# Hybrid SSD and differential-attention layer on one core: two short pauses written into TensorE's planned order

## The chip, the cores and the metric

The kernel runs on one core of a Trainium2 chip: TensorE (matmuls, its weight loads listed apart), VectorE, ScalarE, GpSimd (POOL) and the DMA queues, of which SyncE issues nearly all. The metric is the device time of one execution in microseconds; the time of a kernel is the median of its runs.

## The reference

One encoder layer over x (1024 tokens x 1024 features, float32). After a layer norm h, one projection gives z, x/B/C, step sizes, q, k, v and a gate g (6688 columns). One branch is a bidirectional Mamba-2 scan with a gated RMS norm. The other is differential attention, 8 heads, two softmax maps per head, value width 128:

```
scores = einsum(q, k) * 64**-0.5 - slope[h] * |t - s|
w      = softmax(map 0) - lam * softmax(map 1)
o      = einsum(w, v)                                   # (tokens, 8, 128)
o      = rms_norm(o, subln_g) * (1 - lam_init) * silu(g)
```

Both branches are joined, projected by w_out (2048 x 1024), added to 2**0.25 * h and layer-normed.

## The kernel before

Products of float32 accuracy are made of three float32r products, of high and low parts: hi*hi, hi*lo, lo*hi. All of TensorE's instructions are issued in one order that a small planner, the class `Loom`, works out while the program is built. Each piece of work is a generator, a lane; `LANES` (line 29) gives it a rank and a margin. What a lane yields says when it wants to go on:

- tiles: when the planner's model has them ready, plus the lane's margin;
- a function: when it is true;
- a float: that long after TensorE's planned free time.

`run` (line 103) takes the lane that is due first; of those due by TensorE's planned time, the one with the lowest rank. The model counts 512 x 0.000417 + 0.003 us for a 512-column float32r product and 0.107 for a transpose. Only TensorE's order is pinned by it in this stage: the order of VectorE, ScalarE and GpSimd, and the place of each tile in its pool, are made by the framework's own scheduler from the program.

The attention stage runs from about 420 to 1110 us. Its lanes:

- `fill` (rank 9): the input projection. A block is 128 output columns; for each half of the tokens (512) it accumulates 8 triples of products in one PSUM bank, yielding between triples. The head's blocks come as q, k, v, gate, head after head, so that the projections of later heads fill TensorE between the pieces of the attention of earlier ones.
- `scores` (rank 4): for a block of 128 queries, four products of 512 columns for the two maps and four with the low part of k, to two PSUM tiles of their own pool (`a_s`); VectorE then adds the distance term and finds the minimum, ScalarE takes the exponential.
- `combine` (4.125): the two maps are scaled and subtracted, on POOL and VectorE.
- `values` (4.25): the map (tile `p`) is transposed in two groups of four, each into a bank, copied as high part `wh` (ScalarE) and low part `wl` (VectorE); after every second block of queries 24 products with the values follow. Only when a block's second group has been split does the lane let `scores` go on.
- `v_tail` (rank 3, margin 0.4; lines 935 to 943): a half of a v block is copied from its bank to `vc` by ScalarE; this lane transposes it in four pieces into a bank, from which ScalarE makes `vh` and VectorE `vl`.
- `finish` (4.2, margin 2; lines 1070 to 1100): once per head and half of the tokens, the RMS norm of `o`. ScalarE squares `o`, the square is split in `osh` and `osl`, two products with ones sum it over the 128 partitions into a bank (`pms`), VectorE reads the bank into `msq`, ScalarE takes logarithm and exponential (`rt`), VectorE polishes, and `o` goes to DRAM by four DMAs. `done` counts the halves; it frees the gate buffers of the head before last, and for head 6 it opens the pool of the output projection.

The banks: `bank` (line 247) takes one of four PSUM banks (tag `bk`). `fill`, `values`, `v_tail` and `finish` all use it; the lanes ask for their bank before they yield for it. The last stage, `project_out`, begins in the last head's attention, when the input projection has no blocks left.

Of the kernel before, what the change touches and what calls it, by code (L numbers as in the profile page):

```python
# [216 lines left out]
def hybrid_layer_kernel(  # L217
# [29 lines left out]
    def bank(shape=(128, 512)):  # L247
        return pm.tile(shape, F32, name="bk", bufs=4)

    def dma(dst, src):  # L250
        SP.dma_start(dst, src)

    def transpose(dst, src, n=128):
        T.transpose(dst, src, ident[:n, :n])
# [630 lines left out]
    heads_ = [Head(h) for h in range(8)]  # L885

    def free_since(h, what, n):

        if h == 0 and what != "done":
            return None  # L890
        if h < 2:
            return lambda: state["open"]
        return lambda: getattr(heads_[h - 2], what) == n
# [31 lines left out]
    def proj_v(h):  # L925
        H = heads_[h]

        def evac(half, ps):
            if half == 0:
                H.vh = H.pool().tile([128, NCH, 128], F32R, name="vh")  # L930
                H.vl = H.pool().tile([128, NCH, 128], F32R, name="vl")
            vc = (att["ap"] if h else late["sq"]).tile([128, 512], F32, name="vc", tag="zr", bufs=2)
            A.copy(vc, ps)

            def tail():
                pt = bank((128, 4, 128))
                yield (vc, pt)
                for j in range(4):
                    transpose(pt[:, j, :], vc[:, 128 * j:128 * j + 128])
                t = slice(4 * half, 4 * half + 4)  # L940
                A.copy(H.vh[:, t, :], pt)
                V.tensor_sub(H.vl[:, t, :], pt, H.vh[:, t, :].bitcast(F32))
                H.v += 1
            loom.add(tail(), "v_tail")
        queue.append(Block(V0 + 128 * h, evac, free_since(h, "summed", 4)))
# [87 lines left out]
    def values():  # L1033

        for _ in range(64):
# [31 lines left out]
            if n:  # L1067
                loom.add(finish(H, H.o, tb // 4))

    def finish(H, o, half):  # L1070

        h = heads_.index(H)
        osq = ap.tile([128, 512], F32, name="osq")
        A.activation(osq, o, AF.Square)
        hi = ap.tile([128, 512], F32R, name="osh", tag="rt")
        lo = ap.tile([128, 512], F32R, name="osl", tag="msq")
        A.copy(hi, osq)
        V.tensor_sub(lo, osq, hi.bitcast(F32))
        pms = bank()
        yield (lo, pms)  # L1080
        T.matmul(pms, ones_r, hi, start=True, stop=False)
        T.matmul(pms, ones_r, lo, start=False, stop=True)
        rt = ap.tile([128, 512], F32, name="rt")
        ms = ap.tile([128, 512], F32, name="msq")
        V.tensor_scalar(ms, pms, 1.0 / 128, EPS, op0=ALU.mult, op1=ALU.add)
        A.activation(rt, ms, AF.Ln)
        A.activation(rt, rt, AF.Exp, scale=-0.5)
        yield rt
        V.tensor_mul(ms, ms, rt)
        V.tensor_mul(ms, ms, rt)  # L1090
        V.tensor_scalar(ms, ms, -0.5, 1.5, op0=ALU.mult, op1=ALU.add)
        yield lambda: H.g == 1
        P.tensor_mul(o, o, H.gate[:, 512 * half:512 * half + 512])
        V.tensor_mul(rt, rt, ms)
        yield o
        V.scalar_tensor_tensor(o, o, sub8, rt, op0=ALU.mult, op1=ALU.mult)
        for j in range(4):
            dma(y_dram[4 * half + j][:, 8 + h, :], o[:, 128 * j:128 * j + 128])
        H.done += 1
# [219 lines left out]
```

## Time and profile before

| | |
|---|---|
| median of 3 runs | 1236.25 us (1234.08 to 1236.62) |
| profiled execution | 1231.77 us, its span 1230.1 us |
| mean granted TensorE clock | 0.992 |
| VectorE, ScalarE, POOL busy, share of the span | 73%, 57%, 38% |
| DMA | 98.02 MB, mean 80 GB/s |

Times are in microseconds. PE is TensorE's matmuls and PEld its weight loads, DVE VectorE, ACT ScalarE. A row of the timeline has the start, the duration, the engine, a helper's line (140 for all), the operation, `out<-in` by tile names, the shapes and the count of merged instructions; in brackets the idle time of that engine before it and what ended it. All tiles of `bank` are called `bk`, so their readers and writers tell them apart: `bk<-hh,whi`, `bk<-hl,whi` and `bk<-hh,wlo` are one triple of `fill`, `bk<-ident,vc` the transposes of v, `bk<-ident,p` those of the maps, `bk<-osh,ones_r` and `bk<-osl,ones_r` the products of the norm, `sc<-kk,q` and `sc<-kl,q` the scores. Matmuls are pipelined, so what one costs is read from one start to the next.

### The profile page before, as it was taken

Reading aid. Unit: us, or ns where it says so; the run is one execution under the profiler, and the core shown is the slowest. Engines: PE = TensorE matmul, PEld = TensorE weight load, DVE = VectorE, ACT = ScalarE, POOL = GpSimd, SP = SyncE. Lnnn points to the kernel's source line nnn. Section 1 sums busy time; section 2 is a strip of 40 time slices with the busy share of each in tenths; the row PEclk is TensorE's granted clock in tenths of the full one; section 3 lists DMA queues with packets and bytes.
Section 4 is the critical chain, followed back from the end, with each engine's and each line's share of the span. In section 5 each row is a group of like instructions: output and inputs, shape, how many; then the busy total and the mean of one; then the engine's idle time right before and its main releaser. Section 6 shows DMA issues by size and latency. Waiting matters only on the chain. (4 is left out here: it accounts for less than half of the span.)

```text
span 1230.1 us, 16472 instructions
## 1 busy us (share of the span) xinstructions
PE 1173.1 (95%) x5881; PEld 920.5 (75%) x5881; DVE 898.5 (73%) x1303; ACT 701.8 (57%) x1281; POOL 471.2 (38%) x404
## 2 busy tenths in 40 slices
PE   5999999999999999999999999999999997999997
PEld 3777667788668777778787777877777776788885
DVE  6686876767876568788788887887878888762334
ACT  4557578734577466566655657556656686552221
POOL 7412564323753223323332333233232429352354
PEclk9999999999899999999999999999999999999999
DMA  6113345622344531111111121121111263023221
GB/s 199 30 36 112 86 129 158 185 64 65 94 122 144 153 113 43 28 47 48 26 48 39 43 53 26 35 52 36 43 35 43 79 210 116 26 77 121 78 86 60
DMA packets 107590, 98.02 MB, mean 80 GB/s; under 512 B 9364, under 2 KB 79349, under 8 KB 107509
## 3 DMA queue, kind: packets, MB, share of 16 engines
q1 hardware_dynamic: 107509, 96.98, 27.4%
q8 instruction: 46, 0.75, 0.3%
q14 instruction: 35, 0.29, 0.1%
HBM read 75.85 MB, written 16.91 MB: 75 GB/s over the span
## 5 line engine op out<-in xcount | busy, mean ns | idle before, releaser
L140 PE MATMUL bk<-hh,whi 128*128 128x512 f32 x832 | 352.8, 424 | 0.9 <-DVE yt L140 0.3
L140 PE MATMUL bk<-hl,whi 128*128 128x512 f32 x832 | 327.2, 393 | 3.2 <-POOL hl L140 2.8
L140 PE MATMUL bk<-hh,wlo 128*128 128x512 f32 x832 | 328.2, 394 | 0.0
L140 ACT ACTIVATE p<-p,nm 128x1024 f32<-128x1024 f32 x128 | 146.8, 1148 | 127.7 <-DVE nm L140 126.9
L140 POOL TENSOR_TENSOR wlo<-wst,whi 128x512 fp32r<-128x512 f32 x104 | 159.0, 1534 | 144.6 <-ACT whi L140 122.2
L140 POOL TENSOR_SCALAR p<-p,rs 128x1024 f32<-128x1024 f32 x56 | 64.4, 1150 | 352.7 <-DVE rs L140 293.0
L140 PEld LDWEIGHTS bk<-hh,wlo 128*128 128x128 f32 x832 | 156.7, 188 | 35.0
L140 PEld LDWEIGHTS bk<-hh,whi 128*128 128x128 f32 x832 | 157.6, 189 | 33.1 <-issue 5.7
L140 PEld LDWEIGHTS bk<-hl,whi 128*128 128x128 f32 x832 | 157.8, 190 | 32.8 <-POOL hl L140 5.5
L140 DVE CUSTOM_DVE_ANT_0 p<-sc,dist 128x1024 f32<-128x1024 f32 x128 | 151.3, 1219 | 20.2 <-PE sc L140 19.6
L140 DVE SCALAR_TENSOR_TENSOR p<-p,rs,p 128x1024 f32<-128x1024 f32 x64 | 127.7, 1995 | 21.3 <-POOL p L140 18.0
L140 ACT CAST wh<-bk 128x512 fp32r<-128x512 f32 x128 | 74.2, 580 | 50.5 <-PE bk L140 49.9
L140 DVE TENSOR_TENSOR wl<-bk,wh 128x512 fp32r<-128x512 f32 x128 | 87.1, 684 | 15.6 <-ACT wh L140 13.6
L140 ACT CAST whi<-wst 128x512 fp32r<-128x512 f32 x104 | 64.1, 621 | 42.5 <-PE bk L140 34.3
L140 PE MATMUL bk<-ident,p 128*128 128x128 f32 x512 | 78.3, 275 | 2.6 <-ACT o L140 2.2
L140 PEld LDWEIGHTS bk<-ident,p 128*128 128x128 f32 x512 | 61.0, 140 | 26.1 <-issue 5.5
L140 ACT ACT_TABLE_LOAD x46 | 59.0, 1283 | 28.9 <-DVE t L140 17.3
L140 PE MATMUL bk<-wh,vh 128*128 128x256 f32 x256 | 74.7, 292 | 0.0
L140 PE MATMUL sc<-kk,q 128*128 128x512 f32 x256 | 72.3, 394 | 0.0
L140 PE MATMUL bk<-wl,vh 128*128 128x256 f32 x256 | 72.0, 281 | 0.0
L140 PE MATMUL bk<-wh,vl 128*128 128x256 f32 x256 | 72.0, 281 | 0.0
L140 PEld LDWEIGHTS bk<-xt,t 128*128 128x128 f32 x256 | 45.0, 190 | 24.7 <-issue 16.0
(217 smaller groups left out, 2161.3 us busy)
## 6 DMA issues: line engine op xcount, KB each, us to landing
wst<-in_w_in_dram SPq DMA_DIRECT2D x104, 256.0 KB, 3.0
t<-acs_d SPq DMA_DIRECT2D x64, 256.0 KB, 3.4
ws<-in_w_out_dram SPq DMA_DIRECT2D x32, 256.0 KB, 3.8
ys<-yd SPq DMA_DIRECT2D x32, 256.0 KB, 3.0
xb<-in_x_dram SPq DMA_DIRECT2D x8, 512.0 KB, 6.5
zd<-zs SPq DMA_DIRECT2D x16, 256.0 KB, 3.0
gz<-zd SPq DMA_DIRECT2D x16, 256.0 KB, 3.1
yd<-ys SPq DMA_DIRECT2D x16, 256.0 KB, 2.8
```

Of the source, the lines that this page charges most:

```text
L140: r = f(*args, **kw)
```

## The change

```diff
@@ -935,6 +935,7 @@
             def tail():
                 pt = bank((128, 4, 128))
                 yield (vc, pt)
+                yield 0.4
                 for j in range(4):
                     transpose(pt[:, j, :], vc[:, 128 * j:128 * j + 128])
                 t = slice(4 * half, 4 * half + 4)
@@ -1078,6 +1079,8 @@
         V.tensor_sub(lo, osq, hi.bitcast(F32))
         pms = bank()
         yield (lo, pms)
+        if H is not heads_[7]:
+            yield 0.8
         T.matmul(pms, ones_r, hi, start=True, stop=False)
         T.matmul(pms, ones_r, lo, start=False, stop=True)
         rt = ap.tile([128, 512], F32, name="rt")
```

When the lane of the transposed values has come up in the planner's order, it now steps back and is due again 0.4 us after TensorE's planned free time; so do the norm's products, with 0.8 us, in all heads but the last. Every instruction stays as it is. The program after the change holds the same instructions; TensorE's order, and with it what the scheduler makes of the other engines, can differ.

## Rows read from the trace of the kernel before

**Rows 1.** The page, part 1: busy time and share of the span.
```profile
PE 1173.1 (95%) x5881; PEld 920.5 (75%) x5881; DVE 898.5 (73%) x1303; ACT 701.8 (57%) x1281; POOL 471.2 (38%) x404
```

**Rows 2.** Sums by stretch: length, PE, PEld, DVE, ACT, POOL, granted clock, DMA.
```profile
430.00:980.00 550.00, 548.18 (x2945) 433.32 (x2944) 442.39 (x661) 334.83 (x582) 170.69 (x125) 1.00 0.18 46
...
1040.00:1046.00 6.00, 5.29 (x12) 4.02 (x13) 3.05 (x6) 0.29 (x1) 5.84 (x5) 0.50 0.16 44
```

**Rows 3.** Waits, 430 to 980: total us, times, longest.
```profile
PEld bk L140 <- ACT vc L140: 5.5, 13, 0.6
...
PEld bk L140 <- DVE osl L140: 3.7, 10, 0.5
```

**Rows 4.** Timeline, TensorE: a steady triple, transposes, and the triple behind.
```profile
476.00 0.40 PE L140 MATMUL bk<-hh,whi 128*128 128x512 f32 x1
...
476.70 0.60 PE L140 MATMUL bk<-ident,p 128*128 128x128 f32 x4
477.06 0.48 PE L140 MATMUL bk<-hh,whi 128*128 128x512 f32 x1
...
477.84 0.39 PE L140 MATMUL bk<-hh,whi 128*128 128x512 f32 x1
```

**Rows 5.** Timeline, TensorE: transposes of v, first half, head 1.
```profile
492.30 0.39 PE L140 MATMUL bk<-hh,wlo 128*128 128x512 f32 x1
...
492.82 0.42 PEld L140 LDWEIGHTS bk<-ident,vc 128*128 128x128 f32 x4 [0.56 <-ACT vc L140]
...
494.01 1.09 PE L140 MATMUL sc<-kk,q 128*128 128x512 f32 x4
```

**Rows 6.** Timeline, TensorE: around the transposes of v, second half, head 1.
```profile
502.20 0.48 PE L140 MATMUL bk<-hh,whi 128*128 128x512 f32 x1
...
504.20 1.08 PE L140 MATMUL sc<-kk,q 128*128 128x512 f32 x4
```

**Rows 7.** Timeline, TensorE: transposes of v, second half, head 7.
```profile
993.53 0.66 PE L140 MATMUL bk<-ident,vc 128*128 128x128 f32 x4 [0.57 <-ACT vc L140]
```

**Rows 8.** Timeline, TensorE: transposes of v, second half, head 0.
```profile
425.75 0.42 PEld L140 LDWEIGHTS bk<-ident,vc 128*128 128x128 f32 x4 [1.39 <-ACT vc L140]
```

**Rows 9.** Timeline, TensorE: norm products, first half, heads 0 and 1.
```profile
481.61 0.47 PE L140 MATMUL bk<-osh,ones_r 128*128 128x512 f32 x1
...
483.71 1.08 PE L140 MATMUL sc<-kk,q 128*128 128x512 f32 x4
...
561.52 0.47 PE L140 MATMUL bk<-osh,ones_r 128*128 128x512 f32 x1
...
563.50 0.86 PE L140 MATMUL sc<-kk,q 128*128 128x512 f32 x3
```

**Rows 10.** Timeline, TensorE: norm products, second half, heads 0 and 5.
```profile
521.30 0.40 PE L140 MATMUL bk<-osh,ones_r 128*128 128x512 f32 x1
...
521.77 0.19 PEld L140 LDWEIGHTS bk<-osl,ones_r 128*128 128x128 f32 x1 [0.52 <-DVE osl L140]
...
522.38 0.19 PEld L140 LDWEIGHTS bk<-hh,whi 128*128 128x128 f32 x1 [0.41 <-DVE wl L140]
...
523.18 1.09 PE L140 MATMUL sc<-kk,q 128*128 128x512 f32 x4
...
524.87 0.66 PE L140 MATMUL bk<-ident,p 128*128 128x128 f32 x4
...
920.21 0.40 PE L140 MATMUL bk<-osh,ones_r 128*128 128x512 f32 x1
...
923.71 0.55 PE L140 MATMUL bk<-ident,p 128*128 128x128 f32 x3
```

**Rows 11.** Timeline, VectorE and TensorE: a pass over the scores; the next half block.
```profile
526.12 1.22 DVE L140 CUSTOM_DVE_ANT_0 p<-sc,dist 128x1024 f32<-128x1024 f32 x1
...
530.52 0.48 PE L140 MATMUL bk<-hh,whi 128*128 128x512 f32 x1
```

**Rows 12.** Timeline, TensorE's weight loads: the longest wait for a bank.
```profile
1040.71 0.29 PEld L140 LDWEIGHTS bk<-oh,oyh 128*128 128x128 f32 x1 [4.15 <-DVE wl L140]
```

## The prediction, made before the change was run

> **What bounds the kernel now.** I read the page first: TensorE is busy 95% of the span [rows 1]. Then the sums by stretch, for the stage in which nearly all of the changed code runs: between 430 and 980 us TensorE is busy 548.18 of 550.00 us, VectorE 442.39, ScalarE 334.83, all at full clock [rows 2]. The reader is to see that in this stage TensorE's order is the time: an instruction on it that waits delays all behind it, and VectorE has a fifth of the stage free, so it does not take over at once when TensorE gains a little. Third, the waits of that stage: TensorE's weight loads wait 13 times for the copy `vc` (5.5 us) and 10 times for `osl`, the low half of the squares (3.7 us) [rows 3]. These are what the two edits touch. Last, the timeline at each of their 32 places, read by starts (from one start to the next), since ends of matmuls are modelled.
>
> The units of the sum come from [rows 4]: a projection triple (three 512-column products of `fill`) takes 0.70 us (476.00 to 476.70), so a product 0.23; four transposes 0.36 (476.70 to 477.06); a triple right behind transposes 0.78 (477.06 to 477.84), so 0.08 more.
>
> **The change part by part.** Nothing is added to or taken from any engine; 16 groups of four transposes and 14 pairs of products (the last head's two are excluded) may move behind other TensorE work. To know behind what, I followed the planner: a projection triple counts 3 x (512 x 0.000417 + 0.003) = 0.65 us in its costs, four transposes 0.43, and among lanes that are due the lowest rank goes first (v_tail 3, scores 4, combine 4.125, finish 4.2, values 4.25, fill 9).
>
> *First half's transposes, heads 1 to 7 (7 places).* Now: the triple before them begins its last product at 492.30, the load waits 0.56 us for `vc` and starts at 492.82, then comes one triple, and the scores start at 494.01: 1.71 us [rows 5]. With 0.4 the lane yields, a triple (0.65 in the plan) passes, then the transposes (rank 3) go ahead of the scores. `vc` is there by 492.82, and the triple fills 492.53 to 493.23. After: 0.23 + 0.70 + 0.36 + 0.08 = 1.37. Gain 0.34 x 7 = 2.4 us.
>
> *Second half's transposes, heads 1 to 6 (6 places).* Now triple, transposes, triple, scores: 502.20 to 504.20, 2.00 us [rows 6]. After, both triples first: 0.78 + 0.70 + 0.36 + 0.08 = 1.92. Gain 0.08 x 6 = 0.5.
>
> *Second half of head 7.* The transposes stand between scores and a value product group and idle TensorE for 0.57 us [rows 7]. The value products (rank 4.25, 24 of them) are due and go first. Gain 0.6. *Head 0* gains nothing: its first group only swaps with transposes that are ready; its second waits 1.39 us [rows 8] in a stretch where no other lane is due, and since the yield counts from TensorE's planned free time, which lies before the lane's old due time, it is picked again at once.
>
> *Norm products, first half of the rows, heads 0 to 6 (7 places).* Now transposes, `osh`, `osl`, two triples, scores: 481.61 to 483.71, 2.10 us, in four heads, and 561.52 to 563.50, 1.98 us, in three [rows 9]. 0.8 is passed after two triples (1.30); the scores lane opens only behind them. After: 0.78 + 0.70 + 0.46 = 1.94. Gain 4 x 0.16 + 3 x 0.04 = 0.8.
>
> *Norm products, second half, heads 0 to 5 (6 places); the largest term.* Now `osh` starts at 521.30, `osl` waits 0.52 us for VectorE, then the first triple of a new block waits 0.41 for `wl` on VectorE, which has to empty a PSUM bank; scores start at 523.18 and end at 524.87: 3.57 us; in head 5 it is 920.21 to 923.71, 3.50 [rows 10]. In the planner, after the yield the triple goes (0.65, the 0.8 isn't over), then `values` resumes without TensorE work, which opens `scores` (rank 4, ahead of finish), and only then the products: triple, eight score products, `osh`, `osl`. The open price is the triple's bank. `osh` finds one at 521.30 without a wait, the triple behind it does not. If banks go in the order of first use, the triple takes the one that `osh` has now, and the products, 2.4 us later, take the bank that `wl` frees: 0.70 + (524.87 - 523.18) + 0.46 = 2.85, gain 0.72 (last place 0.65), about 0.69. If the triple keeps its bank, it waits to 522.38 as now and the two products come on top: a loss of 0.46. These are the two ends; I take the gain, because the row that is nearest, `osh` at 521.30, shows a bank that is free and a tile that takes it only when first written. 0.69 x 6 = 4.1. Second half of head 6: scores first, no wait there now or then: 0.
>
> *Sum:* 2.4 + 0.5 + 0.6 + 0.8 + 4.1 = 8.4 us. What hides nothing is late next: the transposed values aren't needed until the head's first value products, tens of us on; the norm's rest frees the gate buffer two heads on. Of VectorE's, ScalarE's and POOL's orders the change fixes none; they follow. No DMA is added; those of `o` leave up to 2.4 us later, and nothing in these heads reads them.
>
> The profiled execution took 1231.77 us (span 1230.1): 1223.4 after. It lies 4.48 below the median of the runs, 1236.25; against that, **1227.9 us**.
>
> **Rivals.**
>
> *A, the bank stays.* The triple waits for `wl` wherever it stands. For it: the 0.41 us wait in each of the six [rows 10]. Against: the bank that `osh` found. Then 8.4 - 6 x (0.69 + 0.46) = 1.5 us remain: 1234.7, no measurable change (0.2%, some 2.5 us, is what runs of this kernel can tell from none).
>
> *B, slower: the norm's own bank comes back late.* The products now end behind the scores, so VectorE reads them (`msq`) behind the two passes over the scores, the second of which starts at 526.12 and takes 1.22 [rows 11]. The next half block wants a bank at 530.52; after the change some 0.7 earlier, 529.8. With passes 1.2 earlier `msq` ends near 526.8, 3.0 us to spare. If VectorE's order puts it behind more than that, TensorE stops at all six places. It turns the result from 8.4 / 6 = 1.4 us a place, that is from an end of `msq` near 531.2; with the longest wait for a bank in this trace, 4.15 us [rows 12], it costs 24.9: 1252.8. For it: only four banks; against: the 3.0 us.
> The Trainium skill speaks against the change here: its page "PSUM — Partial Sum Buffer", Summary: rules for kernel authors, says to "evacuate promptly", and the edit empties this bank later. The trace agrees that banks are scarce at this place (the 0.41 us [rows 10]); by that rule alone this rival's 1252.8 would be the time.
>
> *C, the end of the attention stage.* At 1040.71 TensorE has waited 4.15 us for a bank that VectorE's `wl` frees [rows 12], and between 1040 and 1046 its granted clock is 0.50, the lower of its two levels (1.2 GHz), with 5.29 us busy: 2.65 us more than at full clock [rows 2]. Head 6's norm moves behind scores just before, and the conversions and residual loads around it are reordered. If the wait goes, 4.15 + 2.65 = 6.8 us more are gained: 1221.1; if one like it is added: 1234.7.
> "TensorE: Matmul & The Clock Gate", Part 1 (the HAM clock gate), of the Trainium skill says that the array's clock halves after idleness and returns with activity; the rows agree here, the half clock following the longest wait. By it the 0.2 to 0.6 us waits removed give back no clock (the stage has 1.00), and the 2.65 hangs on the 4.15.
>
> *D, the change does not do what it says:* `osl` and `vc` are late because VectorE and ScalarE run behind, and their waits reappear at the next bank. For it: wait behind wait at 521.77 and 522.38; against: VectorE's free fifth. Then about 0: 1236.
>
> **Numbers.** Forecast 0.65 (own range 1225 to 1231.5: one term of the sum gone, or the wait for each half again as large); C with gain 0.09, with loss 0.03; A 0.08; B 0.08; D 0.07. Faster by over 0.2%: 0.65 + 0.09 + 0.01 of A = 0.75. Within: 0.07 + 0.07 + 0.02 = 0.16. Slower: 0.08 + 0.01 = 0.09. The range leaves out B and holds the others: from C's gain less the runs' spread, 1219.5, to 1236.5.
>
> **What would show it.** Right: no TensorE wait for `vc` in heads 1 to 7 nor for `osl`; at the six places the order triple, eight scores, `osh`, `osl`, with no wait for `wl` before the triple; 430 to 980 us shortened by nearly 8 us with VectorE's sum unchanged. A is shown by the triple waiting first; B by a half block's first triple waiting for `msq`; C by the wait and the clock near 1040. The prediction is wrong if those waits are gone and the stage is not shorter.

## The result, and the profile after

The changed kernel takes 1251.72 us (median of 4 runs, 1249.06 to 1253.73) where the kernel before, run beside it, takes 1235.16 (1233.73 to 1236.62): the ratio is 1.0133, 95% interval 1.0115 to 1.0151. It is slower by 16.6 us; the prediction was 1227.9, faster. The profiled execution took 1253.3 us with a span of 1251.6, 21.5 us more than the one before. TensorE has the same 5881 products to do:

```profile
PE 1177.8 (94%) x5881; PEld 926.6 (74%) x5881; DVE 893.9 (71%) x1303; ACT 705.6 (56%) x1281; POOL 478.2 (38%) x404
```

Against [rows 1], TensorE is busy 4.7 us longer and the rest of the 21.5 us is idleness. The sums by stretch (columns as in [rows 2]) show it in the attention stage, and show that VectorE didn't take over:

```profile
430.00:980.00 550.00, 535.17 (x2871) 425.43 (x2871) 420.40 (x635) 328.78 (x565) 169.19 (x121) 1.00 0.18 46
1040.00:1046.00 6.00, 3.23 (x7) 2.34 (x8) 5.96 (x11) 5.12 (x9) 2.85 (x3) 0.65 0.91 299
```

TensorE now does 2871 products in the 550 us that held 2945; all engines do less. The waits of TensorE's weight loads in that stretch (total us, times, longest; "issue" means that the profile names no releaser) name part of what is late:

```profile
PEld bk L140 <- issue: 21.4, 51, 1.9
...
PEld bk L140 <- ACT vc L140: 6.7, 6, 1.4
PEld bk L140 <- DVE osl L140: 6.2, 3, 2.1
PEld bk L140 <- DVE wl L140: 3.6, 8, 0.5
```

The prediction said that the waits for `vc` and `osl` would be gone. They are fewer than in [rows 3], 6 for 13 (one of the six is head 0's of [rows 8], which now falls into the stretch) and 3 for 10, but longer, 1.4 and 2.1 us for 0.6 and 0.5, and their totals have not fallen. At head 3, second half, and at the next head's transposed values the weight loads and VectorE show:

```profile
780.89 0.19 PEld L140 LDWEIGHTS bk<-osh,ones_r 128*128 128x128 f32 x1
783.14 0.19 PEld L140 LDWEIGHTS bk<-osl,ones_r 128*128 128x128 f32 x1 [2.06 <-DVE osl L140]
...
823.28 0.42 PEld L140 LDWEIGHTS bk<-ident,vc 128*128 128x128 f32 x4 [0.81 <-ACT vc L140]
```

```profile
779.10 2.32 DVE L140 SCALAR_TENSOR_TENSOR p<-p,rs,p 128x1024 f32<-128x1024 f32 x1 [1.13 <-POOL p L140]
781.34 1.75 DVE L140 TENSOR_TENSOR osl<-osq,osh 128x512 fp32r<-128x512 f32 x1
```

`osl` stands behind the combination of the maps on VectorE, so the norm's second product waits 2.06 us, four times what it waited in [rows 10], although it was put later. These two waits recur once in each head from head 3 to head 5.

*The order.* I counted in both traces the projection triples that start between one `osh` product and the next. Before: 31, 33, 31, 33 and so on, to the end of the projection. After: 30, 39, 32, 33, 33, 40, 30, 34, 30, 34, 30, 36, 12. Another count says the same without the moved products: how many triples more than before have started when a block of scores begins. It is 0 for eleven blocks, but for -5 at the eighth; from the twelfth on it is 3 to 7, and from head 3 to head 6 8 to 19. So the change didn't only move the 30 groups that have a pause; the planner drew another order for the whole stage.

*Where the 21.5 us lie*, by the starts of products in the two traces. TensorE's order is the same up to a product behind which the next begins at 426.35 us (before 420.97): 5.4, before any moved group; the experiments come back to it. From there to head 0's second `osh` 1.8, of which one triple, 0.7, is work done early. From that `osh` (528.46; [rows 10]: 521.30) to head 5's (945.41; 920.21) 416.95 us and not 398.91: 18.0 more, of which 15 triples at 0.70 us, 10.5, are work that was done early, and 7.5 is waiting. The remainder is only 3.7 us shorter although it has those 16 triples, 11.2 us, less to do: 7.5 of waiting and of a lower clock (see rival C below). 5.4 + 1.1 + 7.5 + 7.5 = 21.5.

### The profile page after: what moved, and what is told of

Read it like the earlier page. It is cut to its first block, busy times and chain, and to the rows that moved or that the text cites. A ratio compares the mean times of both kernels' runs of the same rounds, so it can differ in the third digit from the quotient of the medians.

```text
span 1251.6 us, 16473 instructions
## 1 busy us (share of the span) xinstructions
PE 1177.8 (94%) x5881; PEld 926.6 (74%) x5881; DVE 893.9 (71%) x1303; ACT 705.6 (56%) x1281; POOL 478.2 (38%) x404
## 5 line engine op out<-in xcount | busy, mean ns | idle before, releaser
L140 POOL TENSOR_SCALAR p<-p,rs 128x1024 f32<-128x1024 f32 x56 | 67.2, 1201 | 331.4 <-DVE rs L140 331.3
L140 DVE SCALAR_TENSOR_TENSOR p<-p,rs,p 128x1024 f32<-128x1024 f32 x64 | 112.9, 1764 | 22.7 <-POOL p L140 20.2
```

The lines of the kernel that those rows point to most:

```text
L140: r = f(*args, **kw)
```

## The experiments

Ratios are to the kernel before, run on the same chip in the same rounds. "us a head" is the time from head 0's second `osh` to head 5's in the profiled execution, divided by five; where the number of triples in it differs from 320 it is given. The ratios are as recorded; they differ from the quotients of the medians by up to 0.1%.

| | median us | ratio, 95% interval | us a head |
|---|---|---|---|
| before (beside e1 to e4) | 1234.23 | | 79.8 |
| the change (first runs) | 1251.72 | 1.0133, 1.0115 to 1.0151 | 83.4 (335 triples) |
| e1_v_only | 1235.82 | 1.0011, 0.9997 to 1.0024 | 79.8 |
| e2_norm_only | 1252.0 | 1.0144, 1.0126 to 1.0162 | 83.3 (327) |
| e3_local | 1233.86 | 0.9998, 0.9986 to 1.001 | 79.6 |
| e4_after_back | 1251.55 | 1.0144, 1.0124 to 1.0163 | 83.8 (336) |
| before (beside e5 to e8) | 1234.45 | | |
| e5_no_first_norm | 1234.03 | 1.0005, 0.9992 to 1.0017 | 79.6 |
| e6_less_vector | 1228.69 | 0.9958, 0.9943 to 0.9972 | 79.2 |
| e7_low_on_vector | 1227.94 | 0.9951, 0.9935 to 0.9967 | 78.7 |
| e8_phase | 1262.01 | 1.0232, 1.0212 to 1.0252 | 85.9 (348) |
| before (beside e9 to e12) | 1234.6 | | |
| e9_pause_05 | 1233.26 | 0.9997, 0.9983 to 1.0011 | 79.2 |
| e10_other_phase | 1234.42 | 1.0002, 0.9989 to 1.0015 | 79.2 (324) |
| e11_after_low_on_vector | 1241.5 | 1.0065, 1.0042 to 1.0088 | 82.0 (335) |
| e12_both | 1228.63 | 0.9952, 0.9935 to 0.997 | 78.7 |

**e1 and e2: each edit alone.**

```diff
 e1:
                 yield (vc, pt)
+                yield 0.4
 e2:
         yield (lo, pms)
+        if H is not heads_[7]:
+            yield 0.8
```

> Only the pause of 0.4 behind the transposed values; the norm's lines are as before. Theory P (the loss is not in the moved groups: the planner's whole order of the attention stage was re-drawn, and that comes with the norm's pause): TensorE's order keeps the 31 and 33 projection triples between the norm's products that it has before, so the predicted terms 2.4 + 0.5 + 0.6 = 3.5 us come: 0.3% faster than before, about 1231.7 us. Rival G (a moved group costs by itself, as it holds one of the four banks for longer): slower, with 14 of the 32 groups moved some 4 to 8 us.

> Only the pause of 0.8 ahead of the norm's products, in all heads but the last. Both theories: slower. P: nearly the whole loss, 13 to 17 us (about 1248 to 1252), with the number of projection triples between two of the norm's products no longer 31 and 33 from head 0's second half on. G: only its share of the groups (14 of 32), 6 to 9 us.

The whole loss comes with the norm's pause. The values' pause keeps the count of 31 and 33 triples, and doesn't cost; but it brings none of its 3.5 us either, a miss of theory P. In e1's trace the 13 waits for `vc` are gone (the one that is left is head 0's of [rows 8], which falls into the stretch here), and the first row of these, of its waits from 430 to 980 us, tells where the time went:

```profile
PEld bk L140 <- DVE osl L140: 6.1, 10, 0.9
...
PEld bk L140 <- ACT vc L140: 1.4, 1, 1.4
```

`osl` is waited for 6.1 us and not 3.7 [rows 3], up to 0.9 at a time: TensorE came earlier to the norm, and VectorE didn't. In e2's trace, from 635 us on, three long waits recur in each head, here around head 3. The first triple of a new half block, and the transposed values (weight loads, then VectorE):

```profile
737.71 0.19 PEld L140 LDWEIGHTS bk<-hh,whi 128*128 128x128 f32 x1 [1.80 <-issue]
...
748.09 0.42 PEld L140 LDWEIGHTS bk<-ident,vc 128*128 128x128 f32 x4 [1.43 <-ACT vc L140]
```

```profile
735.11 1.76 DVE L140 TENSOR_TENSOR osl<-osq,osh 128x512 fp32r<-128x512 f32 x1
736.90 0.69 DVE L140 TENSOR_TENSOR kl<-bk,kk 64x512 fp32r<-64x512 f32 x1
```

The triple starts 0.12 us after `kl` ends, which empties the bank of the k block; `kl` stood behind the norm's `osl`. The profile names no releaser here; the times fit the bank. The third is 1.81 us, for the transposes of a map whose combination has just ended. The counts are 31 and 33 again there, but at the scores the projection is 3 to 7 triples ahead of the kernel before: the same alternation at another offset, and 83.1 us a head.

**e3 and e4: the moves without the new order, and the new order without the moves.** For both, TensorE's order was written out as a list of lanes, which replaces the planner's choice (the function `run`). With the list recorded from the kernel before and not edited (e6 and e7 below), all 5881 products come in its order. e3 edits that list, e4 the list recorded from the changed kernel; but for the moved groups, TensorE's order in e3 is product for product that of the kernel before, and in e4 that of the changed kernel.

```diff
-            best = None
...
-            ln = best[1]
+            ln = next(l for l in self.lanes if l[2] == ORDER[self.turn])
+            self.turn += 1
+            assert ln[4] is None or ln[4]()
```

> TensorE's order of the kernel before, written out, with the 14 + 14 groups moved by hand exactly to where the prediction put them, and nothing else of TensorE's order changed (no pause in the planner). P: the prediction's own sum, 8.4 us faster: about 1226.8 us, no waits for vc or osl in heads 1 to 6. G: the moved groups cost by themselves: not faster, 1235 to 1252. Between: if the 3.7 us of the norm's second halves doesn't come, 1231.

> TensorE's order of the changed kernel, written out, with each of the paused groups put back to where its lane came up before the pause: the moves are undone, the re-drawn order around them stays. P: still slower than before by 12 to 20 us (about 1247 to 1255). G: the loss goes, 1235.

e4 keeps the whole loss with not one group moved; e3 has all the moves and no loss. So the loss is the redrawn order, and G falls. But e3 has no gain either: 0.3 us where P had 8.4. Its trace settles each term. From one fixed point to the next, on average over the places of a term: the first-half transposes, with the projection ahead and the scores behind, take 7.69 us and not 8.05 (0.36 gained, 0.34 predicted); the second-half ones 3.60 and not 3.64 (0.04; 0.08); head 7's second half gains 0.64 (0.6); the norm's second halves take 4.40 and not 4.99 (0.59; 0.69). The norm's first halves take 4.97 and not 4.09 in heads 1 to 6: 0.84 to 0.93 lost a place, 5.3 in all, where 0.04 to 0.16 were to be won (head 0's stays at 4.16). Together 2.5 + 0.2 + 0.6 + 3.5 - 5.3 = 1.5 us, and the interval of the ratio goes from 1.7 us faster to 1.2 slower. At such a place, head 3's, in the kernel before (VectorE, then TensorE's loads):

```profile
721.22 2.31 DVE L140 SCALAR_TENSOR_TENSOR p<-p,rs,p 128x1024 f32<-128x1024 f32 x1
723.45 0.67 DVE L140 TENSOR_TENSOR kl<-bk,kk 64x512 fp32r<-64x512 f32 x1
724.05 0.67 DVE L140 TENSOR_SCALAR msq<-bk 128x512 f32<-128x512 f32 x1
...
724.77 0.42 PEld L140 LDWEIGHTS bk<-ident,p 128*128 128x128 f32 x4 [0.39 <-DVE msq L140]
```

and in e3:

```profile
724.54 2.32 DVE L140 SCALAR_TENSOR_TENSOR p<-p,rs,p 128x1024 f32<-128x1024 f32 x1
...
727.38 0.67 DVE L140 TENSOR_TENSOR wl<-bk,wh 128x512 fp32r<-128x512 f32 x1
...
728.10 0.42 PEld L140 LDWEIGHTS bk<-ident,p 128*128 128x128 f32 x4 [1.26 <-DVE wl L140]
...
728.83 0.69 DVE L140 TENSOR_SCALAR msq<-bk 128x512 f32<-128x512 f32 x1
```

Before, the map's transposes behind the scores took the bank that `msq` had just emptied. With the norm later, `msq` is later, and they wait 1.26 us for another bank. This is the prediction's rival B, a bank that comes back late, at a place where it wasn't looked for. In e3's waits it is most of one row (seven of the 13), against 4.7 us in 12 before:

```profile
PEld bk L140 <- DVE wl L140: 10.9, 13, 1.5
```

**e5: e3 without that place.** In e3's list, the seven moves of the norm's first halves are taken back.

```diff
     move the transposed values behind the next triple (or value products)
-    move the norm's first halves behind two triples
     move the norm's second halves behind triple and scores
```

> The written-out order of e3 without its seven moves of the norm's first halves (they stand as in the kernel before); the 14 groups of transposed values and the second halves of the norm are moved. Theory Q (in e3 the first halves gave the gain back at their own place: the bank of the norm came free 4.8 us later, and the transposes of the map waited 0.84 us for another bank, 7 times 0.84 = 5.9 us): 5 to 7 us faster than before, about 1228. Rival W (VectorE's and ScalarE's own chain paces a head at 79.8 us, and whatever TensorE gains at one place it waits again at the next osl or wl): no change, 1233 to 1236.

W holds, Q falls. The second halves and the values gain about 1.0 us a head as in e3, and the wait is at the next thing that VectorE hands over, the norm's first half. The waits of e5, its loads and its VectorE there:

```profile
PEld bk L140 <- DVE osl L140: 6.2, 7, 1.1
```

```profile
878.88 1.66 DVE L140 TENSOR_TENSOR osl<-osq,osh 128x512 fp32r<-128x512 f32 x1
...
879.49 0.19 PEld L140 LDWEIGHTS bk<-osh,ones_r 128*128 128x128 f32 x1
...
880.59 0.19 PEld L140 LDWEIGHTS bk<-osl,ones_r 128*128 128x128 f32 x1 [0.90 <-DVE osl L140]
```

Before there was no wait at this place in heads 1, 3 and 5 and one of 0.2 us in the others. From head 4's second `osl` to head 5's first VectorE takes 39.91 us (838.97 to 878.88), where in the kernel before it took 40.12 (839.00 to 879.12): what TensorE wins in between hardly shortens VectorE's round.

**e6 and e7: VectorE relieved, TensorE's order untouched.** Both run on the list of the kernel before.

```diff
 e6:
-        V.tensor_mul(ms, ms, rt)
-        V.tensor_mul(ms, ms, rt)
-        V.tensor_scalar(ms, ms, -0.5, 1.5, op0=ALU.mult, op1=ALU.add)
...
-        V.tensor_mul(rt, rt, ms)
 e7:
-    def split_w(st, hi, lo, act=A):
+    def split_w(st, hi, lo, act=A, sub=P):
         act.copy(hi, st)
-        P.tensor_sub(lo, st, hi.bitcast(F32))
+        sub.tensor_sub(lo, st, hi.bitcast(F32))
...
-                b.w.append(split_w(st, hi, lo))
+                b.w.append(split_w(st, hi, lo, sub=V if b.col >= Q0 and (b.col - Q0) // 128 % 8 else P))
```

> TensorE's order of the kernel before, written out and unchanged; left out is the polish of the norm's inverse root (four of VectorE's operations of 0.42 to 0.69 us per half head, 2.5 us; the inverse root is then as ScalarE's logarithm and exponential give it). W: the waits for osl, wl and msq shrink, 0.5 to 1 us a head, 4 to 8 us faster than before (1227 to 1231). Rival Q (TensorE's own time is the bound, VectorE's idle fifth is real): within 2 us of before.

> TensorE's order of the kernel before, written out and unchanged; the low parts of the weights (wlo) of heads 1 to 7 are made by VectorE and not by POOL. In the profile before, VectorE's combination of the maps takes 1.28 us when POOL is idle and 2.30 beside POOL's wlo (1.98 us each), and osl takes 1.72 where wl, of the same size, takes 0.68. If that is what makes osl late (W), VectorE loses 56 x 0.69 = 39 us of work to do and wins about as much back, osl comes earlier, and the time goes down by 2 to 6 us. Q: no change, or slower by what the added operations delay.

Both times came out as W has it: with the same order on an engine that was "busy 548.18 of 550 us" the kernel is 5.2 us faster (e6) and 6.1 us (e7). The busy share hid that TensorE also waits for VectorE; a busy time of pipelined matmuls with modelled ends covers waits of half a microsecond, as the 0.52 us in [rows 10]. The sums between 430 and 980 us (columns as in [rows 2]), e6, then e7:

```profile
430.00:980.00 550.00, 548.62 (x2957) 436.23 (x2956) 395.68 (x612) 339.30 (x584) 174.76 (x125) 1.00 0.18 48
430.00:980.00 550.00, 547.42 (x2965) 438.11 (x2964) 441.18 (x722) 340.68 (x592) 85.72 (x73) 1.00 0.19 48
```

e6 takes work off VectorE alone. Its waits are not quite those that W named: `msq`'s 2.8 us stay, `osl`'s fall from 3.7 to 3.0 only, and 0.41 of the 0.54 us a head come at the transposed values, whose waits for `vc` are gone. ScalarE makes `vc` behind an exponential that waits for the minimum `nm` from VectorE; without the four operations that wait is 0.59 us shorter (ScalarE at head 1, before, then e6, where the scheduler also puts one `wh` a head behind the second exponential):

```profile
489.44 1.16 ACT L140 ACTIVATE p<-p,nm 128x1024 f32<-128x1024 f32 x1 [2.13 <-DVE nm L140]
...
492.20 0.57 ACT L140 COPY vc<-bk 128x512 f32<-128x512 f32 x1
```

```profile
492.65 1.15 ACT L140 ACTIVATE p<-p,nm 128x1024 f32<-128x1024 f32 x1 [1.54 <-DVE nm L140]
...
495.40 0.59 ACT L140 COPY vc<-bk 128x512 f32<-128x512 f32 x1
```

e7 leaves VectorE's sum as it was and halves POOL's, so it doesn't tell how much of its gain comes from shorter operations on VectorE and how much from an earlier POOL. The waits for `vc` in heads 1 to 6 are gone in it too, with ScalarE's order as before. VectorE's busiest groups between 500 and 900 us, before:

```profile
L140 DVE SCALAR_TENSOR_TENSOR p<-p,rs,p 128x1024 f32<-128x1024 f32 x40 | 82.0, 2050 | 13.0 <-POOL p L140 13.0
L140 DVE TENSOR_TENSOR wl<-bk,wh 128x512 fp32r<-128x512 f32 x80 | 54.4, 684 | 9.0 <-ACT wh L140 7.7
L140 DVE TENSOR_TENSOR osl<-osq,osh 128x512 fp32r<-128x512 f32 x10 | 17.2, 1722 | 0.0
```

and in e7 (the number after the bar is busy time in us, then the mean in ns):

```profile
L140 DVE SCALAR_TENSOR_TENSOR p<-p,rs,p 128x1024 f32<-128x1024 f32 x41 | 57.6, 1405 | 8.2 <-POOL p L140 7.3
L140 DVE TENSOR_TENSOR wlo<-wst,whi 128x512 fp32r<-128x512 f32 x41 | 28.0, 684 | 0.2
...
L140 DVE TENSOR_TENSOR osl<-osq,osh 128x512 fp32r<-128x512 f32 x10 | 11.7, 1172 | 0.0
```

VectorE got 28.0 us of work more and won 24.4 + 5.5 back; e7's wait for `osl` is down to this, and e7 is the fastest kernel of the study, with e12:

```profile
PEld bk L140 <- DVE osl L140: 1.2, 4, 0.5
```

**e8 and e10: the step between projection and attention, with no group moved.** One pause in the lane of the scores, once in the whole kernel.

```diff
 e8:
                 yield lambda: count["s"] - count["t"] < 2
+                if h == 0 and tb == 5:
+                    yield 2.0
 e10:
                 yield lambda: count["s"] - count["t"] < 2
+                if h == 0 and tb == 7:
+                    yield 4.0
```

> The kernel before with one pause and nothing else: the planner lets the scores of head 0's sixth block come up 2.0 us later. None of the 32 places of the change has a pause. Theory P (the loss is the lost step between projection and attention, wherever it is lost): projection triples between the norm's products no longer 31 and 33, and 10 to 17 us slower than before (1245 to 1252). Rival G: 0 to 2 us slower.

> The kernel before with one pause and nothing else, as e8, but of 4.0 us ahead of the scores of head 0's eighth block. The projection gets 10 triples ahead there and then keeps 31 and 33 in turn. P1 (the step of the kernel before is the only good one): 10 to 25 us slower. P2 (what costs is not the step lost once but an order that goes on with waits for VectorE after it): less than 10 us slower, 1232 to 1244.

e8 is the slowest kernel of all, 27.6 us above before where P had 10 to 17, by one pause of 2 us: its triples between norms go 34, 36, 33, 42, 35, 30, 32, 39 and never settle, and the projection gets up to 36 triples ahead. e10 goes 37, 37 and then 31 and 33 in turn, at the scores mostly 8 triples ahead, which is one half block, and is as fast as before: P1 falls, P2 holds. Its rounds are even shorter, 78.7 us a head from head 1 on; against that, its second `osh` comes 5.1 us later in the stage.

**e9: a shorter pause.**

```diff
-            yield 0.8
+            yield 0.5
```

> Both pauses, but 0.5 in place of 0.8 ahead of the norm's products (0.4 behind the values as in the change). A projection triple counts 0.65 in the planner, so 0.5 lets one triple pass and 0.8 two. Theory P: the step is kept (31 and 33 triples in turn between the norm's products), and by W the moved groups bring nothing: 1232 to 1237, within 0.3% of before. Rival G (a later place of the norm's products costs, by its size): half of the change's loss or more, 1242 to 1250.

As expected: 31 and 33 are kept, and the time is the same. In the trace no wait for `osl` is left between 430 and 980 us, nor one for `vc` in heads 1 to 7, and a head takes 0.6 us less (79.2), so W's "bring nothing" is too strong for this order; the span of the whole execution is 0.6 us shorter, which the runs can't tell from none. Nearly the same move, past one triple in the plan and not two, has no cost: at the scores the projection is 0 triples ahead, but for one block in eight where it is 5 behind, as head 0's eighth in the changed kernel.

**e11 and e12: e7's relief under the new order and under the moved groups.** The edits are e7's, on the changed kernel's list and on e5's.

> TensorE's order of the changed kernel, written out and unchanged; the low parts of the weights of heads 1 to 7 are made by VectorE and not by POOL, as in e7. W and P together (the new waits are for a VectorE that runs later than the planner counts, beside POOL): 8 to 15 us of the 17 come back, 1237 to 1244. If the waits lie in the order itself: only the 6.5 us that e7 gave: about 1245, or less.

> e5 and e7 together: the 14 groups of transposed values and the second halves of the norm moved by hand, and the low parts of the weights made by VectorE. W (with VectorE relieved, what TensorE gains at a place is not waited again): 2 to 5 us below e7's 1227.9, so 1223 to 1226. If e7 has taken away the same waits already: the same as e7 within 1.5 us.

e11 gives back 10 us, of which e7's 6.1 to 6.5 came to the old order as well. The redrawn order costs 1241.5 - 1227.9 = 13.6 us even so, and 82.0 us a head. So VectorE's length beside POOL explains some 3 of its 16.6 us by the medians, which the intervals of the three ratios don't tell from none. The time came out as expected, but the reason given for it was wrong: the rest is in the order. Of its waits in 430 to 980 us that have a named releaser, two rows are the largest:

```profile
PEld bk L140 <- ACT vc L140: 5.2, 5, 1.5
PEld bk L140 <- DVE osl L140: 3.0, 3, 1.0
```

e12 is the same as e7 within 0.7 us, so W's 2 to 5 us didn't come: the waits that the moves could take away are gone already.

*The first 420 us.* The orders of all engines are the same there in all kernels, but for `wlo` in e7, e11 and e12, and the product behind TensorE's last common one begins at 420.97 us in the profile before, 420.74 in e4, 421.52 in e5, and at 426.35 after, 425.87 in e1, 425.22 in e2. So the 5.4 us that the first comparison showed there are taken as variation between executions and no part of the change's cost: 21.5 - 5.4 = 16.1, near the 16.6 of the medians.

## Why the prediction was wrong, step by step

**The step that failed** is in "The change part by part", its first paragraph: "To know behind what, I followed the planner", at one head, place by place, and then multiplied by 7, 6, 7 and 6. It took for granted that behind each place the order goes on as before. (Its "32 places" are 30 with a pause; it left the last head's two norms out of the sum, not out of the count.) Head 0's places came out as described. But a greedy planner with one shared model carries every delay on. As its program reads, the norm's products came later in the model, and VectorE's slots behind them too; as the traces show, the scores behind head 0 came up at other triples, and between its second half and head 1's first the projection did 39 triples and not 33. From then on evacuations of other blocks meet the norm. That this order is what costs is shown by e4, the loss with no group moved, and e3, all moves and no loss; e2 shows that the norm's pause brings it, and e8 that another pause can. D held that the change might not do what it says; that it might do much more was no rival.

**The sum of 8.4 us** fails as well, even with the order held (e3). The terms for the transposed values (2.4; 0.36 a place measured) and for the norm's second halves (4.1; 0.59 a place, 3.5) were sized about right at their places. The first halves' 0.8 was wrong in sign (5.3 lost at six of the seven places): I followed TensorE there and not who takes the bank that `msq` frees, though I had done so at the second halves. And without them (e5) the gain is still taken at the next wait for VectorE. The reasoning was "VectorE has a fifth of the stage free, so it does not take over at once": an average over the stage, against a chain (scores, exponential, combination, split) in which VectorE works without a gap just ahead of `osl` (0.0 us idle in its row above), and ScalarE's exponential ahead of `vc` waits for VectorE. Rival D had this mechanism, "their waits reappear at the next bank", at 0.07; with the order held it was the right one.

**The rivals.** B had the right sign and a real mechanism, but not this cause: in the changed kernel no wait for `msq` is named between 430 and 980 us, where before there were 7 short ones. That its 1252.8 lies 1.1 us from the measured 1251.72 is luck. A's bank that stays didn't show in e3, where the triple ahead of the scores doesn't wait. C: at 1040 to 1046 us the clock is 0.65 and TensorE busy 3.23 us; the 4.15 us wait of [rows 12] became two of 2.41 and 2.19. But what C described has a part in the loss, at places that it didn't name: the granted clock also falls between 980 and 1020 and between 1060 and 1110 us (columns as in [rows 2]; before, then after):

```profile
980.00:1020.00 40.00, 34.53 (x179) 26.92 (x177) 33.98 (x52) 36.71 (x61) 13.19 (x10) 1.00 0.64 215
...
1060.00:1110.00 50.00, 48.80 (x250) 39.51 (x249) 37.36 (x53) 29.11 (x51) 20.59 (x13) 1.00 0.21 64
```

```profile
980.00:1020.00 40.00, 35.18 (x184) 27.53 (x183) 36.82 (x52) 30.58 (x54) 17.32 (x11) 0.96 0.48 149
...
1060.00:1110.00 50.00, 47.74 (x241) 37.51 (x240) 38.62 (x59) 28.19 (x48) 24.12 (x17) 0.97 0.20 55
```

By these rows that is some 0.04 x 40 + 0.03 x 50 = 3 us, an estimate. The mean granted clock of its four runs is 0.984 to 0.988, that of the kernel before beside e1 to e4 0.987 to 0.993. It isn't the cause of the 16.6 us: e2 loses as much at 0.989 to 0.992.

**What stays open:** what makes one offset between projection and attention good. 0 triples (before) and mostly 8 (e10) are, 3 to 7 (e2) and up to 19 (after) are not. The waits at the bad ones are shown, a rule for them isn't; nor is it shown why 0.5 us keeps the old order and 0.8 doesn't.

## What to carry to other kernels

A pause in a program that plans its own order is not a move: count something that the order should keep (here the triples between two norms) right after such a change, or write the order out and edit it, before working out gains place by place. Where an engine is "95% busy" and still waits half a microsecond at the same hand-over in every round, relieve the engine it waits for with the order untouched; only if nothing moves is the busy engine the bound. And when a product is put later, follow the bank that it would have returned to whoever took it next.

## What the runs showed of the hardware

VectorE's operations with two inputs in SBUF get slower while POOL works. The combination of the maps took 1.28 us when POOL had just gone idle, in the profile before (POOL and VectorE):

```profile
749.49 1.12 POOL L140 TENSOR_SCALAR p<-p,rs 128x1024 f32<-128x1024 f32 x1 [6.26 <-DVE rs L140]
...
750.64 1.28 DVE L140 SCALAR_TENSOR_TENSOR p<-p,rs,p 128x1024 f32<-128x1024 f32 x1 [0.33 <-POOL p L140]
```

At 721.22 it took 2.31, while POOL made `wlo` (720.70 to 724.68); `osl`, with two SBUF inputs, takes 1.72 on average where `wl`, of the same size with one input in PSUM, takes 0.68. With `wlo` taken off POOL (e7) the means fall to 1.41 and 1.17. Head 1's second `osl` shows it at one place, before (POOL, then VectorE) and in e7, where POOL has nothing to do beside it:

```profile
598.68 2.28 POOL L140 TENSOR_TENSOR wlo<-wst,whi 128x512 fp32r<-128x512 f32 x1
...
599.74 1.78 DVE L140 TENSOR_TENSOR osl<-osq,osh 128x512 fp32r<-128x512 f32 x1
```

```profile
599.92 0.68 DVE L140 TENSOR_TENSOR osl<-osq,osh 128x512 fp32r<-128x512 f32 x1
```

An operation with one input in PSUM and one in SBUF isn't slowed: `kl` at 723.45 took 0.67 us in the middle of POOL's `wlo` (the rows of the kernel before under e3).

The Trainium skill, "SBUF — State Buffer", Who interferes with whom, says that a VectorE instruction with two SBUF inputs contends with a GpSimd instruction that reads SBUF, and that one with at most one SBUF input, outside the two-port modes, doesn't. The rows agree on both: the 1.78 and 0.68 us of `osl`, and the 0.67 of `kl`. Moving an operation from the less busy engine to the busier one was worth 0.5% here (e7), together with what an earlier POOL gives.
